# A hybrid decoder layer on one core: splitting 24 of the mixers' weight sets during the first FFN product

## The chip, the core and the metric

The kernel runs on one core of one Trainium2 chip. The metric is the device time of one launch in microseconds (us). A core has five engines with a queue of their own each: TensorE (PE in the profile, its weight loads PEld), VectorE (DVE), ScalarE (ACT), GpSimd (POOL) and SyncE (SP, which here only issues transfers). Each engine works through its own instructions in the order in which they were recorded, and waits where one of them needs something that isn't there yet.

## What is computed

One layer of a decoder trunk on 1024 tokens of width 1024, all in float32:

```python
x = x + 0.5 * swiglu(rms_norm(x, g_ffn1), w1_gate, w1_up, w1_down)      # d_ff 2816
proj = rms_norm(x, g_mix) @ w_in
c_q, k_a, v_a, k_idx, w_idx, q_b, k_b, v_b, gate_a, gate_b = split(proj)
y_a = dsa_attention(...)            # an indexer scores the keys, the best 256 of each row are attended to
y_b = stick_breaking_attention(q_b, k_b, v_b)
merged = sigmoid(gate_a) * (y_a @ w_o_a) + sigmoid(gate_b) * (y_b @ w_o_b)
x = x + merged @ w_out
x = x + 0.5 * swiglu(rms_norm(x, g_ffn2), w2_gate, w2_up, w2_down)
```

Here `w_in` is 1024 x 4104; 512 columns each of it are `q_b`, `k_b` and `v_b`, 1024 each the two gates.

## The kernel before

Products are done in three passes: both factors are split into a high part (rounded to the matmul's format, `fp32r`) and a low part (the rest), and high by high, high by low and low by high are summed in PSUM. So every operand needs a split before its matmul: a rounding copy on ACT and a subtraction on another engine.

**The FFN products** (`ffn_in`, `ffn_out`) use a seven-product scheme of Strassen's kind on 2 x 2 blocks. `ffn_in` goes over 11 pairs of column blocks `p`; from the second pair on each does two calls of `products` (gate and up), each with seven `mul` of 12 matmuls of 128 x 512. For each call SP loads two weight blocks (`a0r`, `a1r`), DVE forms four sums of them (`s1` to `s4`, lines 456 to 459), ACT rounds seven operands (line 377) and POOL subtracts (line 378). Behind the PE, DVE adds the products up in a ring of 12 tiles, `c` (`a0u`, `a0c`, `a1u`, `asg` and so on), and `finish` writes seven of them per pair to DRAM (`staged`, line 591). Here a scheduler orders the instructions.

**The mixers** stand between the two FFNs and are recorded by a planner, `Weave`: each stream of work is a generator that says before a step which engine it wants and what it needs; the planner keeps a time for each engine and each tile from a cost per instruction, takes the step that can start first (ties by rank), and so writes out one fixed order for all engines. It has two stages, `index` and `attend`. Side by side run:

- `indexer` (PE `psdot`, ACT `relu`, DVE `u`): the scores of six row blocks; blocks 0 and 1 need no selection;
- `topk`: the 256th score of each row is searched bit by bit, 31 bits for each of two groups of three blocks, `groups`; a bit is three counting passes on ACT (line 1136, `junka`) and a few small DVE steps. Then per block a mask is made (lines 1181 to 1194: `gt`, `eq`, `cum`) and stored to `bd`;
- `sticks` and `values`: stick-breaking attention (PE `psz`, ACT `left` and `sa`, DVE a scan and a product, PE transposes `pstT`, ACT and DVE `pt`, PE `psy`);
- `logits`, `soft` and `latent_values`: the sparse attention (PE `psL`, DVE `e`, ACT an exponential at line 1757, DVE a division at line 1760, PE transposes `pspT`, then `pso`). The exponential needs another ACT table, which is loaded once, after the last sigmoid of the gates;
- `fillers`, with the lowest rank: the projections of the mixers' other inputs. A weight set is 128 columns of `w_in` for all 1024 rows. There are 8 for `q_b` and `k_b` (`wqk...`) and 16 for the gates (`wg...`), each used by two times 24 matmuls (`psf`); a half of a gate set ends with a sigmoid on ACT (line 1067, `evg`) and a store. Later the output projections `psob` and `psoa` fill in.

Weight sets come through `weights`, at most three at a time: SP loads 512 KB into one of two `raw` tiles (line 971), ACT rounds all of it (line 974), POOL subtracts (line 976) into a ring of four tiles `w`, two for each set.

## Time and profile before

| | us |
|---|---|
| median of 3 runs (2271.07 to 2281.2) | 2272.52 |
| the profiled execution | 2276.41 |
| span of it, first to last instruction | 2274.6 |
| PE busy | 2183.0 (96%) |
| DVE busy | 1576.1 (69%) |
| ACT busy | 1110.5 (49%) |
| POOL busy | 925.9 (41%) |

The profile counts an engine as busy while one of its instructions runs; times in its views are counted from the start of the span. The granted clock is the share of its full speed that the TensorE had. The first FFN product takes the span up to about 440 us, its second half to about 660, the mixers to about 1500, then follow the output projection and the second FFN.

### The profile page before, as it was taken

What the parts mean: (1) busy time and instruction counts of PE and PEld (TensorE: products, weight loads), DVE (VectorE), ACT (ScalarE), POOL (GpSimd) and SP (SyncE); (2) the same over time, 40 slices, a digit from 0 to 9 for tenths busy, and PEclk for the clock granted to TensorE, in tenths of its full rate; (3) what the DMA queues carried; (4) which work ended last, traced back from release to release, by engine and by line L of the source; (5) the groups of instructions that cost most, each with busy time, mean ns of one, the idle gap of its engine ahead of it and who ended that gap; (6) DMA issues with size and microseconds to landing.
All of it is one profiled execution on the core that took longest, in us unless ns stands there. A gap on an engine that the chain in (4) does not pass through costs nothing.

```text
span 2274.6 us, 30225 instructions
## 1 busy us (share of the span) xinstructions
PE 2183.0 (96%) x10460; PEld 1811.1 (80%) x10460; DVE 1576.1 (69%) x2500; ACT 1110.5 (49%) x2145; POOL 925.9 (41%) x722
## 2 busy tenths in 40 slices
PE   7999999999999899899999799999999999999999
PEld 6788888888879788677788578887878888888877
DVE  5765666678863698477788978853477575757775
ACT  4323232334453368899999656633332323233443
POOL 3555555432253444422323132256255555543233
PEclk9999999999999999999999799999999999999999
DMA  5233333587674343655454532467223333358755
GB/s 168 71 116 92 114 95 113 170 293 257 172 204 131 87 130 92 168 126 116 110 135 128 180 109 90 151 203 251 96 67 112 93 113 94 115 172 287 248 160 184
DMA packets 247930, 330.65 MB, mean 145 GB/s; under 512 B 20576, under 2 KB 154352, under 8 KB 247776
## 3 DMA queue, kind: packets, MB, share of 16 engines
q1 hardware_dynamic: 235264, 288.83, 42.3%
q0 software_dynamic: 12512, 39.89, 4.8%
q8 instruction: 82, 1.34, 0.2%
q14 instruction: 72, 0.59, 0.1%
HBM read 234.78 MB, written 93.88 MB: 144 GB/s over the span
## 4 chain that ended last, share of the span: by engine, by line
PE 70%; DVE 10%; DMA 7%; ACT 6%; issue 5%; POOL 2%; SPq 0%; ACTq 0%; DVEq 0%; POOLq 0%
PE p L677 5%; PE p L678 5%; PE p L676 5%; PE pc L467 3%; PE pc L469 3%; PE pc L468 3%; PE pd L469 3%; PE pd L467 3%; PE pd L468 3%; PE pa L469 3%; PE pa L467 3%; PE pa L468 3%; ACT junka L1136 2%; PE pb L467 2%; PE pb L469 2%
## 5 line engine op out<-in xcount | busy, mean ns | idle before, releaser
L1136 ACT ACTIVATE junka<-u,cand,sig 128x768 bf16<-128x768 f32 (+4 forms) x186 | 183.3, 985 | 10.8 <-DVE cand L1133 9.0
L1577 DVE TENSOR_TENSOR_SCAN left<-left 128x640 f32<-128x640 f32 (+3 forms) x64 | 88.1, 1378 | 3.4 <-ACT left L1569 3.3
L1626 DVE TENSOR_TENSOR pt<-pstT,pt 128x512 fp32r<-128x512 f32 (+1 forms) x96 | 51.1, 551 | 24.8 <-ACT pt L1624 24.2
L1580 DVE TENSOR_TENSOR sa<-sa,left 128x639 f32<-128x639 f32 (+3 forms) x64 | 58.6, 918 | 3.7 <-ACT sa L1571 0.4
L1626 DVE TENSOR_TENSOR pt<-pspT,pt 128x512 fp32r<-128x512 f32 x72 | 46.6, 683 | 19.4 <-ACT pt L1624 19.4
L1680 PE MATMUL pstT<-ident,sa 128*128 128x128 f32 x288 | 47.0, 278 | 11.1 <-DVE sa L1580 5.6
L1624 ACT ACTIVATE pt<-pspT 128x512 fp32r<-128x512 f32 x72 | 39.7, 596 | 36.2 <-PE pspT L1836 35.9
L1757 ACT ACTIVATE e<-e,nm 128x256 f32<-128x256 f32 (+7 forms) x64 | 49.4, 774 | 13.0 <-DVE nm L1752 11.3
L677 PE MATMUL p<-bT,bS 128*128 128x512 f32 x132 | 51.9, 393 | 2.7 <-DVE bT L378 2.7
L678 PE MATMUL p<-bT,bS 128*128 128x512 f32 x132 | 51.7, 394 | 1.0 <-POOL bS L378 1.0
L1680 PEld LDWEIGHTS pstT<-ident,sa 128*128 128x128 f32 x288 | 34.7, 141 | 22.4 <-DVE pt L1626 9.0
L677 PE MATMUL p<-aT,aS 128*128 128x512 f32 x132 | 51.6, 391 | 0.8 <-DVE aT L378 0.8
L1745 DVE CUSTOM_DVE_ANT_0 e<-psL,bias 128x512 f32<-128x512 f32 (+3 forms) x96 | 49.7, 550 | 3.8 <-PE psL L1782 3.8
L1836 PE MATMUL pspT<-ident,e 128*128 128x128 f32 x288 | 42.3, 284 | 10.2 <-DVE e L1760 6.1
L1624 ACT ACTIVATE pt<-pstT 128x512 fp32r<-128x512 f32 (+1 forms) x96 | 46.3, 505 | 11.2 <-PE pstT L1680 10.1
L1490 DVE SCALAR_TENSOR_TENSOR u<-relu,WI,u 128x512 f32<-128x512 f32 (+1 forms) x70 | 47.6, 696 | 4.9 <-ACT relu L1483 3.9
L678 PE MATMUL p<-aT,aS 128*128 128x512 f32 x132 | 50.4, 389 | 0.0
L1483 ACT ACTIVATE relu<-psdot 128x512 f32<-128x512 f32 (+1 forms) x80 | 39.9, 520 | 19.0 <-DVE u L1490 10.3
L1836 PEld LDWEIGHTS pspT<-ident,e 128*128 128x128 f32 x288 | 35.2, 145 | 17.5 <-DVE e L1760 8.9
L1569 ACT ACTIVATE left<-psz 128x512 f32<-128x512 f32 (+2 forms) x96 | 45.9, 502 | 5.5 <-PE psz L1604 5.3
L1899 POOL TENSOR_TENSOR o<-o,gate 128x512 f32<-128x512 f32 x16 | 21.8, 1360 | 65.2 <-ACT o L1894 65.2
L1571 ACT ACTIVATE sa<-psz 128x512 f32<-128x512 f32 (+2 forms) x96 | 46.4, 506 | 0.0
(3067 smaller groups left out, 8319.0 us busy)
## 6 DMA issues: line engine op xcount, KB each, us to landing
aw<-in_w_down_dram SPq DMA_DIRECT2D x33, 512.0 KB, 4.7
bw<-in_w_down_dram SPq DMA_DIRECT2D x33, 512.0 KB, 4.7
a0r<-in_w_gate_dram SPq DMA_DIRECT2D x22, 512.0 KB, 4.3
a1r<-in_w_up_dram SPq DMA_DIRECT2D x22, 512.0 KB, 5.0
b0r<-in_w_gate_dram SPq DMA_DIRECT2D x22, 512.0 KB, 4.1
b1r<-in_w_up_dram SPq DMA_DIRECT2D x22, 512.0 KB, 4.9
x<-in_x_dram SPq DMA_DIRECT2D x16, 512.0 KB, 6.4
gd<-evg POOLq DMA_DIRECT2D x32, 256.0 KB, 6.5
```

The costliest lines, as they stand in the source:

```text
L467: nc.tensor.matmul(ps, a[:, c], b[k][:, HI], start=start and k == 0, stop=False, skip_group_check=True)
L468: nc.tensor.matmul(ps, a[:, c], b[k][:, LO], start=False, stop=False, skip_group_check=True)
L469: nc.tensor.matmul(ps, a[:, l], b[k][:, HI], start=False, stop=k == 3, skip_group_check=True)
L676: nc.tensor.matmul(ps[q][m], S[:, h], T[:, HI], start=p == 0, stop=False)
L677: nc.tensor.matmul(ps[q][m], S[:, h], T[:, LO], start=False, stop=False)
L678: nc.tensor.matmul(ps[q][m], S[:, l], T[:, HI], start=False, stop=p == last)
L1136: nc.scalar.activation(junks[1][:, 0:(i + 1) * P], score[i], AF.Sign, scale=sig[:, b:b + 1], bias=cand.bitcast(F32)[:, b:b + 1], accum_out ...
L1577: nc.vector.tensor_tensor_scan(back, back, back, 1.0, op0=ALU.mult, op1=ALU.bypass)
L1624: nc.scalar.activation(pt[:, off:512], tp[:, off:512], AF.Copy)
L1626: nc.vector.tensor_sub(pt[:, 512 + off:1024], tp[:, off:512], f32(pt[:, off:512]))
L1680: nc.tensor.transpose(tp[:, q * P:(q + 1) * P], A[n + q][:, j * P:(j + 1) * P], ident)
L1836: nc.tensor.transpose(tp[:, q * P:(q + 1) * P], E[n + q][:, j * P:(j + 1) * P], ident)
```

## The change

In the first FFN product, `mul` now calls `beside` behind each of the seven products of a call. Over the first 16 of the 20 calls it takes 48 pieces of 128 x 512 (24 sets, two pieces each) in three slots: a piece is loaded behind one product, rounded on ACT and subtracted on DVE behind a later one, and both parts are stored to DRAM behind the next. `behind` makes each of these wait for the given product's last matmul.

The tiles come out of other rings: the ring `c` has 9 tiles instead of 12 in the loop, `s` 5 instead of 7, and six tiles of 128 x 512 carry the three pieces.

In the mixers these 24 sets are no longer rounded and subtracted: `weights` waits for two tiles of the ring `w` and loads both parts, two transfers of 512 KB instead of one. The last set asked for must have taken its tiles first (`before`). The second selection group is (7, 6, 3) instead of (6, 7, 3).

```diff
-    def ffn_in(nm, R, wg, wu, raw, op, sums, ct, bank, staged, rows, first=None):
+    def ffn_in(nm, R, wg, wu, raw, op, sums, ct, bank, staged, rows, first=None, beside=lambda n, ins: None):
...
-                nc.tensor.matmul(ps, a[:, l], b[k][:, HI], start=False, stop=k == 3, skip_group_check=True)
+                ins = nc.tensor.matmul(ps, a[:, l], b[k][:, HI], start=False, stop=k == 3, skip_group_check=True)
+            return ins
...
-            times(O[a], B[b], ps, start)
+            beside("1567243".index(str(n)), times(O[a], B[b], ps, start))
...
-        sums = of(spool, "s", 7, 512)
+        sums, pair = of(spool, "s", 5, 512), of(spool, "pair", 2, 512, F32R)
...
+            c4, c5, c3, c1 = (of(cpool, f"c{n}", n, 512, F32R) for n in (4, 5, 3, 1))
+            ct = fp(in_turn(*[(f, 1) for f in [c4] * 4 + [c5] * 5]))
+            spare = in_turn((c3, 3), (c1, 1), (pair, 2))
...
+            pieces = [(nm, c) for nm in columns for c in range(0, 1024, 512)]
+            held, points = {}, ((0, 1, 3), (2, 3, 5), (4, 5, 0))
...
+            def beside(n, ins):
+
+                for slot, (split_, store, load_) in enumerate(points):
+                    if n == split_ and slot in held:
+                        nm, c, raw, hi = held[slot]
+                        behind(ins, nc.scalar.activation(hi, raw, AF.Copy))
+                        nc.vector.tensor_tensor(raw, raw, f32(hi), op=ALU.subtract)
+                    if n == store and slot in held:
+                        nm, c, raw, hi = held.pop(slot)
+                        behind(ins, *(nc.sync.dma_start(d[:, c:c + 512], part)
+                                      for d, part in zip(split_of[nm], (f32(hi), raw))))
+                    if n == load_ and pieces:
+                        nm, c = pieces.pop(0)
+                        raw, hi = f32(spare(f"swr{slot}")), spare(f"swh{slot}")
+                        held[slot] = nm, c, raw, hi
+                        behind(ins, nc.sync.dma_start(raw.rearrange("p (k f) -> p k f", f=P),
+                                                      rows_of[:, c // P:(c + 512) // P, columns[nm]:columns[nm] + P]))
...
-    groups = ((5, 4, 2), (6, 7, 3))
+    groups = ((5, 4, 2), (7, 6, 3))
...
+                if nm in split_of:
+                    yield SP, (ws, 2), before
+                    W.parts = ws(nm + "h"), ws(nm + "l")
+                    mark("got" + nm)
+                    for wp, part in zip(W.parts, split_of[nm]):
+                        nc.sync.dma_start(f32(wp), part)
+                    return
```

The planner writes another order for all engines. Three places of it follow. Line numbers in the changed kernel are higher by 1 in `finish`, and by 46 or 47 in the mixers.

ACT, at the end of the search. `junka` is a counting pass of the search, `evg` the sigmoid of a half gate set, `pt` with `pstT` belongs to the sticks, `e` is the exponential. Before:

```order
L1136 ACTIVATE junka,cnt_6038<-u_7809,cand_6043,sig_6039 128x512
L1624 ACTIVATE pt<-pstT 128x384
L974 ACTIVATE ob2h<-ob2r 128x1024
L1624 ACTIVATE pt<-pstT 128x256
L1067 ACTIVATE evg<-psf 128x512
L1624 ACTIVATE pt<-pstT 128x128
L1624 ACTIVATE pt<-pstT 128x512
L1633 ACTIVATE yl<-psy 64x512
L1624 ACTIVATE pt<-pstT 128x384
L1624 ACTIVATE pt<-pstT 128x256
L1639 ACTIVATE yh<-yl 64x512
L1624 ACTIVATE pt<-pstT 128x128
```

After, the last pass stands behind all work of the sticks:

```order
L1183 ACTIVATE junka,cnt_6422<-u_8161,cand_6427,sig_6423 128x512
L1686 ACTIVATE yh<-yl 64x512
L1114 ACTIVATE evg<-psf 128x512
L1228 ACTIVATE gt,cnt_6422<-u_7571,fix_11970 128x1024
L1114 ACTIVATE evg<-psf 128x512
L1020 ACTIVATE ob0h<-ob0r 128x1024
L1114 ACTIVATE evg<-psf 128x512 x2
L1228 ACTIVATE gt,cnt_6422<-u_7882,fix_11970 128x896
L1020 ACTIVATE ob2h<-ob2r 128x1024
L1114 ACTIVATE evg<-psf 128x512
L1802 ACT_TABLE_LOAD
L1804 ACTIVATE e,ssum<-e,nm 128x256 x6
```

In the first list the table load comes next. Before, one sigmoid of a gate stood behind the last search pass, now there are five, and two of the three masks of the second group (`gt` of 1024 and of 896 columns) stand ahead of the first exponential.

PE, between the second and the third group of the sparse attention's transposes. Before, the rows from the products `pso` on:

```order
L1816 MATMUL pso<-pt,kkh 128x512
L1817 MATMUL pso<-pt,kkl 128x512
L1818 MATMUL pso<-pt,kkh 128x512
L1781 MATMUL psL<-kkh,qs 128x256
L1782 MATMUL psL<-kkl,qs 128x256
L1836 MATMUL pspT<-ident,e 128x128 x4
```

After, the first twelve of the rows from the same products on:

```order
L1863 MATMUL pso<-pt,kkh 128x512
L1864 MATMUL pso<-pt,kkl 128x512
L1865 MATMUL pso<-pt,kkh 128x512
L1828 MATMUL psL<-kkh,qs 128x256
L1829 MATMUL psL<-kkl,qs 128x256
L308 MATMUL psob<-ybh_12174,ob0h 128x512
L309 MATMUL psob<-ybl_12178,ob0h 128x512
L310 MATMUL psob<-ybh_12174,ob0l 128x512
L308 MATMUL psob<-ybh_12175,ob0h 128x512
L309 MATMUL psob<-ybl_12179,ob0h 128x512
L310 MATMUL psob<-ybh_12175,ob0l 128x512
L308 MATMUL psob<-ybh_12176,ob0h 128x512
```

Among the first 24 transposes of the sparse attention there are now 33 matmuls of the output projection `psob`, where there were none.

SP in the first FFN product: loads of the weights (`a1r`, `a0r`) and stores of the products. Before, for one pair:

```order
L440 DMA a1r_1461<-in_w_up_dram 128x8x128
L440 DMA a1r_1463<-in_w_up_dram 128x8x128
L440 DMA a0r_1606<-in_w_gate_dram 128x8x128
L440 DMA a0r_1608<-in_w_gate_dram 128x8x128
L591 DMA staged_82<-a0u_1134 128x512
L591 DMA staged_82<-asg 128x512
L591 DMA staged_82<-a0c_1161 128x512
```

After, a stretch of the same pair; `swr` is a piece of a mixers' set, `wg12hd` and `wg12ld` are its two parts in DRAM:

```order
L790 DMA wg11ld<-swr_1225 128x512
L440 DMA a0r_1772<-in_w_gate_dram 128x8x128
L796 DMA swr_1381<-in_w_in_dram 128x4x128
L790 DMA wg12hd<-swh_1260 128x512
L790 DMA wg12ld<-swr_1259 128x512
L440 DMA a0r_1774<-in_w_gate_dram 128x8x128
L592 DMA staged_82<-a0u_1230 128x512
L592 DMA staged_82<-asg 128x512
L796 DMA swr_1415<-in_w_in_dram 128x4x128
L790 DMA wg12hd<-swh_1333 128x512
L790 DMA wg12ld<-swr_1332 128x512
L592 DMA staged_82<-a0c_1264 128x512
```

Loads and stores of the pieces now stand between the loads of the FFN's own weights and between the stores of its products: 18 more transfers for each pair, where there were 11.

## Rows read from the trace of the kernel before

**Rows 1.** The page, part 1: busy us (share of the span) and instructions of each engine.

```profile
PE 2183.0 (96%) x10460; PEld 1811.1 (80%) x10460; DVE 1576.1 (69%) x2500; ACT 1110.5 (49%) x2145; POOL 925.9 (41%) x722
```

**Rows 2.** Windows: length, busy PE, PEld, DVE, ACT, POOL; granted clock, DMA share, GB/s.

```profile
100.00:440.00 340.00, 340.00 (x1501) 281.51 (x1501) 218.13 (x235) 104.44 (x181) 183.93 (x127) 1.00 0.35 111
...
400.00:500.00 100.00, 99.65 (x440) 82.21 (x439) 68.72 (x89) 32.12 (x56) 37.57 (x23) 1.00 0.66 221
...
842.00:1264.00 422.00, 398.77 (x2033) 322.80 (x2033) 319.42 (x584) 384.76 (x816) 134.74 (x140) 0.98 0.50 131
1264.00:1280.00 16.00, 7.42 (x37) 5.87 (x36) 15.45 (x58) 9.00 (x22) 3.98 (x5) 0.79 0.56 200
...
1279.00:1313.00 34.00, 25.03 (x82) 17.91 (x82) 30.60 (x111) 16.75 (x46) 2.17 (x4) 0.65 0.32 95
```

**Rows 3.** Windows of lines 974 (ACT) and 976 (POOL) alone: busy, count.

```profile
842.00:1264.00 422.00, 24.45 (x23) 0.98 0.50 131
...
842.00:1264.00 422.00, 60.78 (x23) 0.98 0.50 131
```

**Rows 4.** Groups of ACT by line, 842 to 1264 us: busy, mean ns, idle before.

```profile
L1136 ACT ACTIVATE junka<-u,cand,sig 128x768 bf16<-128x768 f32 (+4 forms) x186 | 183.3, 985 | 10.8 <-DVE cand L1133 9.0
...
L1624 ACT ACTIVATE pt<-pstT 128x512 fp32r<-128x512 f32 (+1 forms) x91 | 44.2, 509 | 4.8 <-PE pstT L1680 3.8 <-DVE pt L1626 0.8
...
L1067 ACT ACTIVATE evg<-psf 128x512 f32<-128x512 f32 x31 | 18.6, 599 | 0.1
```

**Rows 5.** Timeline of PE: start, duration, instruction [idle before, releaser].

```profile
1250.16 0.39 PE L308 MATMUL psf<-mhi,wg7h 128*128 128x512 f32 x1
...
1250.84 0.39 PE L308 MATMUL psf<-mhi,wg7h 128*128 128x512 f32 x1
...
1268.93 0.66 PE L1680 MATMUL pstT<-ident,sa 128*128 128x128 f32 x4 [3.89 <-DVE pt L1626]
...
1279.59 0.96 PE L1836 MATMUL pspT<-ident,e 128*128 128x128 f32 x2 [4.05 <-DVE nm L1752]
```

**Rows 6.** Timeline of ACT: the last search pass and the table load.

```profile
1261.86 0.89 ACT L1136 ACTIVATE junka<-u,cand,sig 128x512 bf16<-128x512 f32 x1
...
1274.39 1.28 ACT L1755 ACT_TABLE_LOAD   x1
```

**Rows 7.** Groups of DVE and PE by line, 1280 to 1320 us.

```profile
L1187 DVE TENSOR_TENSOR_SCAN cum<-eq 128x896 f16<-128x896 f16 (+2 forms) x3 | 5.5, 1838 | 0.0
...
L1190 DVE TENSOR_TENSOR eq<-cum,gt 128x896 f16<-128x896 f16 (+2 forms) x3 | 1.7, 576 | 0.0
...
L1836 PE MATMUL pspT<-ident,e 128*128 128x128 f32 x24 | 7.6, 417 | 10.2 <-DVE e L1760 6.1 <-DVE nm L1752 4.0
```

**Rows 8.** Timeline of PE, where the fillers' first rounded set comes in.

```profile
764.71 0.80 PE L310 MATMUL psf<-mhi,wqk5200l 128*128 128x512 f32 x1 [3.00 <-POOL wqk5200l L976]
...
769.36 0.60 PE L1400 MATMUL pskt<-ident,kdup 128*128 128x128 f32 x4
...
786.83 0.79 PE L1513 MATMUL psdot<-kih,qsi 128*128 128x512 f32 x1 [6.45 <-ACT relu L1483]
```

**Rows 9.** Timeline of DVE and of the SP queue in the first FFN product.

```profile
193.83 0.69 DVE L458 TENSOR_TENSOR a05s<-a0r,a0r 128x512 f32<-128x512 f32 x1
...
201.35 1.77 DVE L459 TENSOR_TENSOR a05s<-a0r,a05s 128x512 f32<-128x512 f32 x1
...
214.28 0.68 DVE L493 TENSOR_TENSOR a0c<-a0u,pc 128x512 f32<-128x512 f32 x1
...
205.45 0.32 SPq L591 DMA_DIRECT2D staged<-a0u  x1
```

**Rows 10.** DMA issues: line, engine, count, KB each, median us from issue to landing.

```profile
staged<-a0u SPq DMA_DIRECT2D x20, 256.0 KB, 4.0
...
qs<-qad SPq DMA_DIRECT2D x8, 512.0 KB, 4.6
...
wg9r<-in_w_in_dram SPq DMA_DIRECT2D x1, 512.0 KB, 16.8
```

More of the change, by code (lines that the diff above doesn't have):

```diff
@@ L722, in trunk @@
     bd = dram.tile([P, 4224], BF16, name="bd")
+    columns = {f"wg{g}": C_GA + g * P for g in (*range(ND, 2 * ND), *range(ND))}
+    columns.update((f"wqk{base}{pr}", base + pr * P) for pr in range(4) for base in (C_QB, C_KB))
+    split_of = {nm: [dram.tile([P, 1024], F32, name=f"{nm}{part}d") for part in "hl"] for nm in columns}
+    rows_of = w_in[0].rearrange("(k p) f -> p k f", p=P)
     put_high, put_low = nc.scalar.dma_start, nc.gpsimd.dma_start
@@ L785, in trunk @@
             R.second = lambda: R.place(xs[4:8], 1, sums)
-            ffn_in("a", R, w1_gate, w1_up, raw, op, sums, ct, bank, staged[0], range(4), first)
+            ffn_in("a", R, w1_gate, w1_up, raw, op, sums, ct, bank, staged[0], range(4), first, beside)
+            assert not held and not pieces
         hpool.append(tc.tile_pool(name="hpool", bufs=1, side="right"))
@@ L873, in trunk @@
         aux = of(pool, "u", 8, 512)
+        sums = in_turn((sums, 5), (lambda name: f32(pair(name)), 2))
         ffn_out("a", xs, w1_down, raw, op, sums, aux, bank, staged[0], after)
@@ L971, in stream @@
                 nc.sync.dma_start(rv, w[0, k0 * P:(k0 + k) * P, c0:c0 + n].rearrange("(k p) f -> p k f", p=P))
-                yield ACT, raw, (ws, 2)
+                yield ACT, raw, (ws, 2), before
                 wh, wl = ws(nm + "h"), ws(nm + "l")
+                mark("got" + nm)
                 nc.scalar.activation(wh[:, 0:m], raw[:, 0:m], AF.Copy)
@@ L987, in __init__ @@
             def __init__(self, *of):
-                self.todo, self.coming = list(of), []
+                self.todo, self.coming, self.last = list(of), [], None
             def __call__(self):
                 while self.todo and len(self.coming) < 3:
-                    self.coming.append(weights(*self.todo.pop(0)))
+                    last, self.last = self.last, "got" + self.todo[0][-1]
+                    self.coming.append(weights(*self.todo.pop(0), before=last))
                 return self.coming.pop(0)
```

11 lines of the change are left out of this document (7 added, 4 removed).

## The prediction

> **What bounds the kernel now.** I read the page's first part, then windows by stage, then groups and timelines in the stages that the change touches. The PE is busy 96% of the span [rows 1], so a change that leaves its work alone can only win the time in which PE waits or runs at the lower clock. The windows [rows 2] say where that is. In the first FFN product there is none: from 100 to 440 us PE is busy 340.00 of 340 us at full clock, beside DVE 218, ACT 104 and POOL 184. In the mixers there is some. From 842 us (the first counting pass) to 1264 (behind the last) PE is busy 398.8 of 422 us; ACT, with 384.8 us or 91%, is nearly as full, and the search alone takes 183.3 us of it [rows 4]. Behind the last search pass comes a hole: PE is busy 7.4 of 16 us from 1264 to 1280, and from 1279 to 1313 it runs 25.0 of 34 us at a granted clock of 0.65, so that much of that time was at 1.2 GHz instead of 2.4. The reader is to see two things there. The sticks have run out just as the search ends, so PE waits for single results (3.89 us for a `pt`, 4.05 us for the first exponentials [rows 5]). And in the small blocks that follow, PE waits 10.2 us for DVE [rows 7], which is busy 30.6 of 34 us, among other things with the masks of the second group.
>
> **What the change removes.** From 842 to 1264 us ACT rounds 23 sets in 24.45 us, 1.06 us each, and POOL subtracts 23 in 60.78 us, 2.64 us each [rows 3]. Twenty of the 23 are of the 24 sets; the others belong to `wvb` and `ob`. So 20 x 1.06 = 21 us leave ACT in the stretch in which it is 91% full. The other four sets lie before 842 us and count in the second term below.
>
> **First term, the FFN product: 0.** Added are 48 copies on ACT (0.6 us each by the `evg` of [rows 4], an operation of the same 128 x 512, so 29 us), 48 subtractions on DVE, and 144 transfers with 37.7 MB. The work that hides them is PE's: it has no gap in 340 us. Sixteen calls of 19 us (half of the pair's 38) are 305 us, in which DVE has 64% = 196 us of its own work. A subtraction of two SBUF tiles of this size takes 0.69 us, or 1.77 us when POOL works beside it [rows 9]; so the addition is 33 to 85 us, and DVE comes to 75% to 92%. ACT comes to 40%. The traffic rises from 111 GB/s by 124 to about 235; the second half of the FFN moves 221 GB/s with PE at 99.65% [rows 2]. The Trainium skill (SBUF — State Buffer, Who interferes with whom) speaks against the change here: a two-input DVE operation and a POOL operation take the shared ports in turn, each for its whole length. The trace agrees as far as it goes (0.69 against 1.77 us); by that rule alone all 48 would cost the upper price, DVE would stand at 92%, and the term would still be 0. If the cover is gone, each microsecond that a pair's work comes late costs 10 us, once for each of the ten pairs; that is a rival below.
>
> **Second term, the fillers' first set: +3 us.** Now the first `psf` waits 3.00 us for POOL's subtraction [rows 8]. In the changed kernel the set's tiles are free only when the last products with `wvb` have read them, at about 760 us, and then two transfers of 512 KB must land. The nearest row is 4.6 us for 512 KB [rows 10], so PE waits until some 765 to 767 us, and six fillers and six `psq` that stood ahead of the transposes `pskt` now stand behind them, which wait for a DVE result until 769.36 us anyway. Twelve matmuls at 0.227 us are 2.7 us moved behind. Below it is bounded by 0, if the later wait of 6.45 us at 780 us, behind a store, swallows it; above by 6.
>
> **Third term, from the first search pass to the first exponential: -6 us.** ACT's work to the last search pass changes by -21 us, by 7 more `pt` that now stand ahead of it (+3.6 us at 0.51), by 4 sigmoids fewer (-2.4 us at 0.60), and by three copies of the sticks' outputs more (+1.8, priced alike): 384.8 falls to about 367 us. At the same 91% that is 402 us instead of 422, so the last pass, now at 1261.9 us [rows 6], ends about 20 us earlier, near 1244. But behind it stand five half gates instead of one. A half is 24 matmuls 0.227 us apart ((1250.84 - 1250.16) / 3 [rows 5]), 5.4 us; with part of one done, 4.5 x 5.4 = 24.3 us. Then come the table load and the way from it to the first transposes, 1279.59 - 1274.39 = 5.2 us [rows 5, 6]. 1244 + 24.3 + 5.2 = 1273.5, against 1279.6: -6 us. The PE's own work allows it: 406 us busy from 842 to 1280, and one half set of `q_b` or `k_b` more (+5.4), make 1254 without any wait, so the lower bound of the term is -21 us (5 us of waits left). The upper bound is +14: if the search does not end earlier, 1264 + 24.3 + 5.2 = 1293.5.
>
> **Fourth term, the small blocks: -14 us.** From 1279 to 1313 us PE does 82 matmuls in 34 us. Busy 25.0 us at clock 0.65 is worth 16 us at full clock (estimate: product of the two), so 18 us are lost. In the new order 33 matmuls of `psob` stand among the same transposes, 33 x 0.227 = 7.5 us, so PE has 23.5 us to do. DVE had 30.6 us there; two of the second group's three masks are now made ahead of it, under the gates' matmuls, which takes off two thirds of 5.5 + 1.7 us [rows 7], 5 us. DVE then needs about 25.5 us, and I take 27 for the stretch: 3.5 us lost instead of 18, -14.5. Bounds: -18 if nothing is lost, -5 if DVE still sets the pace of the first transposes and PE falls back to the lower clock.
>
> **Sum.** 0 + 3 - 6 - 14 = -17 us on the profiled execution's 2276.4, so 2259.4. That execution lies 3.9 us above the median of the runs shown, 2272.5; on the median the forecast is 2255.5. What lies behind 1313 us keeps its order of transposes and fillers and its work, and I leave it at 0, as the swap of blocks 6 and 7, which keeps each pass and mask.
>
> **Rivals.** *The search keeps its time* (no change). The bits form a chain, pass, compare, next bit, and if that chain and not ACT's load sets the end, the third term is +14: 3 + 14 - 14 = +3, 2275. For it: the passes are spread over the whole stretch. Against: they wait for DVE only 9.0 us in all [rows 4], and ACT is 91% busy. Chance 0.15.
>
> *The sets come late* (a smaller gain). They are now asked for only when the set before last has been used, and with more bytes in flight; one of the old loads took 16.8 us [rows 10]. A set lasts PE 10.9 us in the dense run at the end of the gates. With 17 us per set the last two there would each stall PE 6 us: -17 + 12 = -5, 2267. Against: 4.6 us for the like [rows 10]. Chance 0.08.
>
> *PE becomes the limit* (a larger gain). If ACT was not the only brake and DVE, freed of 20 POOL subtractions of 2.64 us beside it, delivers sooner, the third term goes to -19, the fourth to -17, the second to 0: -36, 2236. The same page of the Trainium skill says so: POOL's hold of the ports falls away. For it: the same kind of operation took 1.77 us instead of 0.69 [rows 9]. Against: DVE is only 76% busy in the stretch. Chance 0.14.
>
> *The FFN product stalls* (slower). The ring `c` has 9 tiles, so the third tile that a pair takes is the one that the pair before gives back with its last store. Now that store is issued at 205.45 us, lands 4.0 us later, and its tile would be wanted at 214.28 [rows 9, 10]: 4.8 us to spare. In the new order two loads and four stores of pieces stand between a pair's stores on SP ahead of it, each with a wait, and SP holds all behind a waiting one. If it lands 4.8 + 4 us later, DVE stands 4 us in each of ten pairs, and with DVE the evacuation of PSUM: +40 - 17 = +23, 2295. It decides from 2.8 us per pair on (28 us, which leaves +11). The Trainium skill (DMA: Bandwidth & Descriptors, Anatomy of one DMA) has the same mechanism: a wait is spent on the issuing sequencer before dispatch. For it also: SP's order shows it. Against: the waits are for products that end at about the times at which SP stood idle there, and the sums of pair 5's weights are formed at 193.83 us, 20 us before the gate product of pair 4 is added up at 214.28 [rows 9]. Chance 0.09.
>
> **How the numbers follow.** The forecast has 0.54; its own range is 2247 to 2264, from the second and fourth terms' bounds and half of the third's. About 0.5% (11 us) is what a measurement of this kernel can tell from no change, so faster means below 2261. Of the forecast 0.46 lies there and 0.08 within the bound; with the larger gain faster has 0.60, with the search and the late sets no change has 0.31, slower 0.09. For 8 in 10 the range takes in the larger gain but for its tail and the search rival: 2237 to 2277.
>
> **What would show it.** The 100 to 440 us window with PE still 100% and DVE above 75%; no rounding of `wqk` and `wg` sets; the last search pass 15 to 25 us earlier than 1262; a dense run of gate matmuls behind it; the first `pspT` a few microseconds earlier; the 34 us of small blocks down to about 27, at a clock above 0.65. Wrong it would be if PE shows gaps in the FFN product, if the last pass stays near 1262, or if PE waits for the sets' transfers.

## The result, and the profile of the changed kernel

The changed kernel takes 2260.69 us (median of 5 runs, 2258.06 to 2263.85) against 2272.52 before: the medians are 11.8 us (0.52%) apart, and the ratio taken over all runs is 0.9938, 95% interval 0.9916 to 0.9961. The forecast was 2255.5 with 2247 to 2264 as its own range. The total came out near it by luck: the first term was 33 us too low, the second and third together 29 us too high.

The profiled execution spans 2262.1 us (2263.85 with what lies around it), before 2274.6. The page of the changed kernel begins as [rows 1] did:

```profile
PE 2172.7 (96%) x10460; PEld 1804.9 (80%) x10460; DVE 1581.0 (70%) x2548; ACT 1110.2 (49%) x2169; POOL 865.4 (38%) x698
```

DVE has its 48 subtractions more, and ACT and POOL have lost the 24 roundings and subtractions of whole sets (ACT has 48 smaller ones instead). The totals of PE, DVE and ACT hardly move; where the time lies has moved. Windows of the changed kernel, columns as in [rows 2]:

```profile
100.00:440.00 340.00, 316.01 (x1353) 256.47 (x1352) 228.04 (x256) 117.86 (x211) 167.06 (x114) 0.98 0.70 205
...
863.00:1251.00 388.00, 377.72 (x1989) 310.82 (x1988) 302.78 (x617) 365.33 (x799) 81.12 (x120) 0.99 0.54 163
...
1280.00:1314.00 34.00, 29.94 (x158) 25.08 (x158) 29.41 (x116) 21.37 (x55) 12.59 (x13) 0.95 0.60 196
```

The first line is the surprise. PE, busy 340.00 of 340 us before [rows 2], now stands for 24 of the same 340 us, while none of its engines is full (DVE 67%, ACT 35%, POOL 49%, transfers 70%). The second line is the search: the window is 388 us long where it was 422, with PE at 97% and ACT at 94%. The last line is the small blocks: at a clock of 0.95 instead of 0.65, PE does 158 matmuls in the time of 82.

To put a number on each stage, four events are read in each kernel: the last sum of the FFN product that takes in `pb` (`a1u<-a1u,pb`), the first and last counting pass of the search (`junka`), and the first transposed exponentials (`pspT`). For the first of them the view by tile gives, before the change and after it (count, shortest, median and longest duration in ns, first and last start):

```profile
L484 DVE TENSOR_TENSOR a1u<-a1u,pb x10: 686/687/689, 107.1 to 449.8; 128x512 f32<-128x512 f32 x10
```

```profile
L485 DVE TENSOR_TENSOR a1u<-a1u,pb x10: 672/674/686, 112.8 to 483.2; 128x512 f32<-128x512 f32 x10
```

The last of the ten moved from 449.8 to 483.2: the FFN product ends 33.4 us late. The other events of the changed kernel, from the timelines of ACT and of PE:

```profile
1248.77 0.80 ACT L1183 ACTIVATE junka<-u,cand,sig 128x512 bf16<-128x512 f32 x1
```

```profile
1280.61 1.94 PE L1883 MATMUL pspT<-ident,e 128*128 128x128 f32 x8 [5.50 <-DVE ri L1806]
```

With 842.0 and 863.0 us for the first pass (before, after) the spans split as follows; the differences add up to the difference of the spans, -12.5 us.

| stretch, us | before | after | difference | forecast |
|---|---|---|---|---|
| start to last `a1u` sum of the FFN product | 449.8 | 483.2 | +33.4 | 0 |
| from there to the first search pass | 392.2 | 379.8 | -12.4 | +3 |
| first search pass to first `pspT` | 437.6 | 417.6 | -20.0 | -6 |
| first `pspT` to the end | 995.0 | 981.5 | -13.5 | -14 |

What PE waits for between 80 and 490 us (engine, tile, line, then who ended the wait: us in total, times, longest):

```profile
PE pc L467 <- DVE a0u L489: 16.4, 8, 4.8
PE pc L467 <- DVE a1u L489: 7.4, 5, 3.8
```

PE wants to put its sixth product into the bank `pc`, and DVE (line 489) hasn't yet added up what lies there. DVE in turn waits, in the same stretch, at line 456, where the next gate and up weights (`a0r`, `a1r`) are first used; the view of that line says how long its engine stood before it:

```profile
  DMA a1r<-in_w_up_dram: 46.9, 8
  DMA a0r<-in_w_gate_dram: 35.8, 7
```

DVE had such waits before the change too, with PE standing 2.9 us in the same stretch, so by themselves they cost it little:

```profile
  DMA a1r<-in_w_up_dram: 41.6, 9
  DMA a0r<-in_w_gate_dram: 25.4, 8
```

PE loses more than the waits. All of them from 80 us on come to 26.3 us, 23.4 more than before; the rest of the 33.4 us is PE at work: about as many matmuls up to the last `a1u` sum (1617 each) keep it busy for 376.9 us instead of 366.9, at a mean granted clock of 0.98 instead of 1.00. Behind the 4.82 us wait below its matmuls start 0.43 us apart instead of 0.227, the lower of its two clock levels (1.2 instead of 2.4 GHz), and the granted clock of 266 to 274 us is 0.57:

```profile
267.94 0.80 PE L467 MATMUL pc<-aT,a05A 128*128 128x512 f32 x1 [4.82 <-DVE a0u L489]
...
268.96 0.63 PE L469 MATMUL pc<-aT,a05A 128*128 128x512 f32 x1
269.39 0.63 PE L467 MATMUL pc<-aT,a05A 128*128 128x512 f32 x1
```

Now a place in the fourth pair, SP's queue first, then DVE, then PE (start, duration, instruction, [idle before it and who ended it]). Before the change, the second half of the same load and DVE's first sum with it:

```profile
149.96 0.37 SPq L440 DMA_DIRECT2D a0r<-in_w_gate_dram  x1
```

```profile
154.49 0.69 DVE L456 TENSOR_TENSOR a04s<-a0r 128x512 f32<-128x512 f32 x1 [3.20 <-DMA a0r<-in_w_gate_dram]
```

After it:

```profile
158.62 0.38 SPq L440 DMA_DIRECT2D a0r<-in_w_gate_dram  x1
159.12 0.52 SPq L796 DMA_DIRECT2D swr<-in_w_in_dram  x1
159.68 0.50 SPq L790 DMA_DIRECT2D wg12hd<-swh  x1
160.88 0.34 SPq L790 DMA_DIRECT2D wg12ld<-swr  x1
161.32 0.42 SPq L440 DMA_DIRECT2D a0r<-in_w_gate_dram  x1
```

```profile
168.63 1.25 DVE L456 TENSOR_TENSOR a04s<-a0r 128x512 f32<-128x512 f32 x1 [4.54 <-DMA a0r<-in_w_gate_dram]
...
173.21 0.68 DVE L787 TENSOR_TENSOR swr<-swr,swh 128x512 f32<-128x512 f32 x1
...
180.81 0.68 DVE L787 TENSOR_TENSOR swr<-swr,swh 128x512 f32<-128x512 f32 x1
181.42 0.67 DVE L489 TENSOR_TENSOR a0u<-a0u,pc 128x512 f32<-128x512 f32 x1
```

```profile
182.15 0.50 PE L467 MATMUL pc<-aT,a03A 128*128 128x512 f32 x1 [1.31 <-DVE a0u L489]
```

Three transfers of pieces stand in SP's order between the two halves of one weight load. They don't part the halves here: 2.7 us lie between them, as before the change (147.25 and 149.96 us). But the second half has landed only at 168.6, 7.3 us behind its issue, where it took 4.5; DVE starts its sums of weights the later, has two subtractions of pieces in the run that follows (1.2 us together, the second directly ahead of the sum that PE needs), and PE stands 1.31 us. So two things take part here, the bytes of the pieces and the subtractions on DVE. DVE also stands for the pieces themselves: before a subtraction it waits for ACT's rounding, and ACT for its product or for the piece:

```profile
DVE swr L787 <- ACT swh L786: 20.4, 14, 6.2
```

The third is the pieces' place in SP's order. SP itself waits for them: a load of a piece (line 796) waits until the slot's earlier piece has been stored. The two longest of sixteen such rows, which come to 62.6 us:

```profile
SPq L796 <- DMA wg0ld<-swr: 9.8, 2, 8.0
...
SPq L796 <- DMA wg6ld<-swr: 6.2, 1, 6.2
```

### The profile page after: what moved, and what is told of

It reads as the page before. It is cut to its first block, busy times and chain, and to the rows that moved or that the text cites. A ratio compares the mean times of both kernels' runs of the same rounds, so it can differ in the third digit from the quotient of the medians.

```text
span 2262.1 us, 30632 instructions
## 1 busy us (share of the span) xinstructions
PE 2172.7 (96%) x10460; PEld 1804.9 (80%) x10460; DVE 1581.0 (70%) x2548; ACT 1110.2 (49%) x2169; POOL 865.4 (38%) x698
## 4 chain that ended last, share of the span: by engine, by line
PE 61%; DVE 8%; ACT 7%; issue 4%; DMA 3%; POOL 1%; SPq 0%; ACTq 0%; DVEq 0%; POOLq 0%
PE p L678 5%; PE p L679 5%; PE p L677 5%; ACT junka L1183 4%; PE pc L467 2%; PE pc L468 2%; PE pc L469 2%; PE pd L469 2%; PE pd L467 2%; PE pd L468 2%; PE pa L469 2%; PE pa L467 2%; PE pa L468 2%; PE psf L308 2%; PE psf L310 2%
## 5 line engine op out<-in xcount | busy, mean ns | idle before, releaser
L1117 POOL DMA_DIRECT2D gd<-evg x32 | 17.9, 558 | 152.5 <-ACT evg L1114 112.6
L787 DVE TENSOR_TENSOR swr<-swr,swh 128x512 f32<-128x512 f32 x48 | 47.2, 984 | 25.4 <-ACT swh L786 20.4
L786 ACT ACTIVATE swh<-swr 128x512 fp32r<-128x512 f32 x48 | 29.9, 624 | 62.9 <-PE pa L469 14.3
L1627 DVE TENSOR_TENSOR sa<-sa,left 128x639 f32<-128x639 f32 (+3 forms) x64 | 48.1, 752 | 3.7 <-ACT sa L1618 0.2
L1530 ACT ACTIVATE relu<-psdot 128x512 f32<-128x512 f32 (+1 forms) x80 | 40.1, 520 | 17.7 <-DVE u L1537 8.7
L1618 ACT ACTIVATE sa<-psz 128x512 f32<-128x512 f32 (+2 forms) x96 | 46.9, 510 | 0.1
```

## The experiments

Twelve kernels were run. Lateness is that of the last `a1u` sum against 449.8 us; times with an interval are medians of several runs on a chip on which the kernel before also ran (its medians there are 2272.5 to 2274.5), the others single runs.

| kernel | time, us | ratio to before | lateness | last `a1u` sum to first pass | search | search to `pspT` | `pspT` to end |
|---|---|---|---|---|---|---|---|
| before | 2272.5 | 1 | 0 | 392.2 | 419.9 | 17.7 | 995.0 |
| changed | 2260.7 | 0.9938 (0.9916 to 0.9961) | 33.4 | 379.8 | 385.8 | 31.8 | 981.5 |
| spread points | 2247.4 | 0.9879 (0.9856 to 0.9902) | 16.5 | 380.1 | 386.3 | 31.9 | 983.9 |
| transfers only | 2249.2 | | 16.9 | 378.3 | 386.2 | 31.8 | 984.1 |
| splitting only | 2235.9 | | 2.1 | 380.4 | 386.0 | 31.8 | 984.0 |
| no pieces | 2230.0 | 0.9809 (0.9792 to 0.9827) | 0.2 | 376.1 | 386.1 | 31.7 | 984.3 |
| spread, no pace | 2301.4 | | 68.8 | 378.4 | 385.9 | 31.9 | 984.8 |
| spread, ACT and GpSimd issue | 2271.7 | 0.999 (0.9979 to 1.0001) | 43.2 | 378.1 | 386.0 | 31.8 | 980.4 |
| spread, ACT issues | 2269.7 | 0.9984 (0.9969 to 0.9999) | 39.4 | 378.9 | 386.0 | 31.8 | 983.8 |
| spread, small transfers | 2231.6 | | 1.3 | 376.1 | 386.4 | 31.8 | 984.4 |
| quiet points | 2249.6 | 0.9888 (0.9872 to 0.9905) | 21.4 | 376.1 | 386.1 | 31.8 | 983.0 |
| spread, ACT's roundings back | 2266.0 | | 17.7 | 380.6 | 407.9 | 16.0 | 992.3 |
| spread, GpSimd's subtractions back | 2262.8 | | 16.8 | 385.9 | 390.6 | 37.8 | 980.1 |
| two slots, 20 sets | 2253.8 | 0.9918 (0.99 to 0.9935) | 15.9 | 383.1 | 389.1 | 31.1 | 978.7 |

**Four kernels on the FFN product.** The first moves the points:

```diff
-            held, points = {}, ((0, 1, 3), (2, 3, 5), (4, 5, 0))
+            held, points = {}, ((0, 1, 4), (2, 3, 6), (4, 5, 1))
```

> Same transfers, same work; only the points move, so that a piece's load stands four or three products (8 to 11 us) behind the stores that free its tiles instead of two (5.4 us). Reading of the changed kernel: the last FFN sum of the first product (a1u<-a1u,pb) ends its series at 483.2 us instead of 449.8, 33.4 us late, and SP's loads of pieces wait some 60 us in all for a store of the slot's earlier piece to land. Theory A (the queue: a load that waits for its slot's store holds SP, and the next pair's gate and up weights come late behind it): SP's waits on stores all but vanish, the lateness falls to under 12 us, the time to about 2238 us. Theory B (traffic: the bytes make every transfer land later, whatever stands in what order): no change, 483 and 2261. Theory C (the 48 subtractions on DVE stand ahead of the sums that PE waits for): no change, 483 and 2261.

The lateness fell to 16.5 us and the time to 2247.4: between what theory A (waits on SP) and what B (bytes) and C (subtractions on DVE) said. SP's waits of a piece's load for a store fell from 62.6 us to 5.7, in six rows of which this is the longest; what is left of the pieces' waits on SP is mostly for the products at which they are paced (44 us in all) and for their own splitting.

```profile
SPq L796 <- DMA wg6ld<-swr: 1.5, 1, 1.5
```

The second leaves out the splitting, the third the transfers, the fourth both:

```diff
-                        behind(ins, nc.scalar.activation(hi, raw, AF.Copy))
-                        nc.vector.tensor_tensor(raw, raw, f32(hi), op=ALU.subtract)
+                        pass
...
-                                      for d, part in zip(split_of[nm], (f32(hi), raw))))
+                                      for d, part in zip(split_of[nm], (raw, raw))))
```

> Leaves out the rounding and the subtraction of the pieces; the unsplit piece is stored twice, so the transfers and their points stay. Theory A: most of the 33.4 us stays, 470 to 483 for the last a1u sum, 2248 to 2261 us; A's waits on stores remain. Theory B: the same. Theory C: the lateness goes, 450 to 455, about 2230 us.

```diff
-    split_of = {nm: [dram.tile([P, 1024], F32, name=f"{nm}{part}d") for part in "hl"] for nm in columns}
+    one = [dram.tile([P, 1024], F32, name=f"one{part}d") for part in "hl"]
+    split_of = {nm: one for nm in columns}
...
+                        if nm == "wg8":
+                            behind(ins, *(nc.sync.dma_start(d[:, c:c + 512], part)
+                                          for d, part in zip(split_of[nm], (f32(hi), raw))))
...
+                        if slot not in kept:
...
+                            nc.sync.dma_start(raw.rearrange("p (k f) -> p k f", f=P), rows_of[:, 0:4, columns[nm]:columns[nm] + P])
+                        held[slot] = (nm, c, *kept[slot])
```

> Leaves out the transfers of all pieces but the first set's stores and one load per slot; 48 roundings and 48 subtractions stay at their points, on three resident pieces, and every set of the mixers is read from the one stored set (the same bytes in the mixers). Theory A and theory B: the lateness goes, 450 to 456, about 2230 us. Theory C: it stays, 475 to 483, about 2255 us.

```diff
-    split_of = {nm: [dram.tile([P, 1024], F32, name=f"{nm}{part}d") for part in "hl"] for nm in columns}
+    one = [dram.tile([P, 1024], F32, name=f"one{part}d") for part in "hl"]
+    split_of = {nm: one for nm in columns}
...
-            pieces = [(nm, c) for nm in columns for c in range(0, 1024, 512)]
+            pieces = [(nm, c) for nm in ["wg8"] for c in range(0, 1024, 512)]
```

> Leaves out all pieces but the two of the first set; every set of the mixers is read from that one stored set, so the mixers do the same work and move the same bytes. It prices the mixers' side alone. All theories: PE full from 100 to 440 us, the last a1u sum at about 450. If the gain of the mixers (12 us before the search, 20 in it, 14 in the small blocks, read from the two traces) stands on its own, the time is about 2272.5 - 46 = 2227 us. If part of it is only waits of the FFN product made up later (work that was late anyway finds the search emptier), the gain is smaller: at 30 us, 2243.

Splitting without the transfers is nearly free: 2.1 us late. Its window has DVE at 80% and PE full:

```profile
100.00:440.00 340.00, 339.81 (x1490) 278.70 (x1490) 270.78 (x283) 125.94 (x223) 186.92 (x126) 1.00 0.36 111
```

Theory C by itself falls. But the transfers without the splitting cost 16.9 us, not 33.4 (less than A and B said), although SP's waits of loads for stores are all there (76.0 us) and DVE stands longer for the weights: 71.4 and 52.3 us at line 456 (46.9 and 35.8 in the changed kernel).

```profile
  DMA a1r<-in_w_up_dram: 71.4, 9
  DMA a0r<-in_w_gate_dram: 52.3, 8
```

So a late weight load costs PE more when DVE has the subtractions to do as well. Whether that is the subtractions' own time or their waits for late pieces isn't separated: with resident pieces the longest such wait is 1.2 us, in the changed kernel 6.2. The costs don't add: transfers 16.9, splitting 2.1, both 33.4. Without either, the kernel takes 2230.0 us, where the kernel before took 2273.5 on the same chip: this is the mixers' gain by itself, 43.5 us against the 17 that were forecast, and it stands on its own. This kernel has the changed kernel's smaller rings too, so 9 tiles in `c` and 5 in `s` cost nothing without the pieces.

**Bytes or order.** Four more kernels start from the spread points.

```diff
-                        behind(ins, *(nc.sync.dma_start(d[:, c:c + 512], part)
-                                      for d, part in zip(split_of[nm], (f32(hi), raw))))
+                        for d, part in zip(split_of[nm], (f32(hi), raw)):
+                            nc.sync.dma_start(d[:, c:c + 512], part)
...
-                        behind(ins, nc.sync.dma_start(raw.rearrange("p (k f) -> p k f", f=P),
-                                                      rows_of[:, c // P:(c + 512) // P, columns[nm]:columns[nm] + P]))
+                        nc.sync.dma_start(raw.rearrange("p (k f) -> p k f", f=P),
+                                          rows_of[:, c // P:(c + 512) // P, columns[nm]:columns[nm] + P])
```

> The spread points, with the order of SP unchanged, but loads and stores of pieces no longer wait for a product (only the rounding does); they wait for their data alone. The spread points alone left the last a1u sum at 466.3 us, 16.5 late, with 57 us of SP's waits on products. Theory A (SP held by waits, now by the pace): a good part goes, 455 to 460, about 2240 us. Theory B (the bytes make the transfers land late): 466 or a little more, 2247 us.

This went against both, 68.8 us late, and its premise was wrong: without the pace the scheduler puts the pieces' transfers earlier in SP's order, so the order did change. (SP's waits on products in the spread kernel, too, are 44 us by the view and not 57.) What it shows is theory A in a strong dose. On SP's timeline the second half of a weight load leaves 7.8 us behind the first, because the piece's load between them waits 6.8 us for a store:

```profile
229.46 0.42 SPq L440 DMA_DIRECT2D a1r<-in_w_up_dram  x1
236.73 0.38 SPq L796 DMA_DIRECT2D swr<-in_w_in_dram  x1
237.21 0.45 SPq L440 DMA_DIRECT2D a1r<-in_w_up_dram  x1
```

```profile
SPq L796 <- DMA wg0ld<-swr: 6.8, 1, 6.8
```

Next, the issue was taken off SP (`put_high` is ACT's `dma_start`, `put_low` GpSimd's):

```diff
-                        behind(ins, *(nc.sync.dma_start(d[:, c:c + 512], part)
-                                      for d, part in zip(split_of[nm], (f32(hi), raw))))
+                        behind(ins, *(put(d[:, c:c + 512], part) for put, d, part in
+                                      zip((put_high, put_low), split_of[nm], (f32(hi), raw))))
...
-                        behind(ins, nc.sync.dma_start(raw.rearrange("p (k f) -> p k f", f=P),
+                        behind(ins, put_high(raw.rearrange("p (k f) -> p k f", f=P),
```

> The spread points, but the pieces' loads and high stores are issued by ACT and the low stores by GpSimd, so that SP carries only the FFN's own transfers; bytes, work and points unchanged. Theory A: SP is free, the last a1u sum comes at 450 to 455, about 2233 us. Theory B: no gain, about 466, 2247 us. A rival to both: ACT's and GpSimd's own waits for products and stores now hold the halves of the operands, then the lateness is moved to the operand tiles and the time is 2245 or more.

The other has `nc.scalar.dma_start` for all three transfers.

> As the run before, with all three transfers of a piece issued by ACT. ACT then also waits for DVE's subtraction before each low store. Theory A: 450 to 458, 2233 to 2240 us. Theory B: 466, 2247 us. If ACT's waits count: over 466.

Both are later than with SP as the issuer, by 27 and 23 us (43.2 and 39.4 against 16.5), so A alone is out, and the outcome is the third reading's. Where ACT issues everything, the trace shows it: a low store waits for DVE's subtraction, and the rounding of an operand that stands behind the store on ACT (line 377) waits with it. There are sixteen such waits, 64.0 us in all, and none in the spread kernel; one of them:

```profile
156.62 0.63 ACT L377 ACTIVATE a03A<-a0r 128x512 fp32r<-128x512 f32 x1 [4.19 <-DVE swr L787]
```

For the kernel in which GpSimd has a share the place of the loss wasn't traced. In the kernel in which ACT issues everything, SP isn't free either: its weight loads waited 40.2 us for pieces' loads.

```profile
SPq L440 <- DMA swr<-in_w_in_dram: 40.2, 7, 8.8
```

The Trainium skill (DMA: Bandwidth & Descriptors, Rules for kernel authors) says that spreading transfers over the issuing engines brings no bandwidth, since all run on the same 16 engines, and saves issue time only. These two runs agree as far as no bandwidth was gained (198 and 200 GB/s from 100 to 440 us, 208 in the spread kernel), and add that the waits that come with a transfer move with its issue.

The last of the four keeps SP's order and its waits for products and takes away the bytes; every set of the mixers is read from the one that is stored whole:

```diff
...
+                        w = 512 if nm == "wg8" else 32
-                        behind(ins, *(nc.sync.dma_start(d[:, c:c + 512], part)
+                        behind(ins, *(nc.sync.dma_start(d[:, c:c + w], part[:, 0:w])
...
+                        raw, hi = kept[slot]
+                        held[slot] = nm, c, raw, hi
+                        behind(ins, nc.sync.dma_start(raw[:, 0:32], rows_of[:, c // P, columns[nm]:columns[nm] + 32]))
```

> The spread points with every transfer of a piece on SP at its place and with its waits, but 32 columns wide instead of 512 (a sixteenth of the bytes; each slot's first load and the first set's stores are whole, and every set of the mixers is read from that set); rounding and subtraction whole. Theory A: SP is held as before, 460 to 466 for the last a1u sum, about 2245 us. Theory B: the lateness goes, 450 to 454, about 2232 us.

1.3 us late, PE full, with as many transfers on SP as in the spread kernel. Theory B holds for what the spread points left over: it needs the bytes. With them go late weights and late pieces alike, so this run doesn't tell which of the two makes DVE late. The view of the DMA issues from 80 to 440 us (KB each, median us to landing), first of the changed kernel, then of this one; before the change the weights landed in 4.2 and 4.9 us:

```profile
swr<-in_w_in_dram SPq DMA_DIRECT2D x48, 256.0 KB, 5.8
a0r<-in_w_gate_dram SPq DMA_DIRECT2D x18, 512.0 KB, 4.9
a1r<-in_w_up_dram SPq DMA_DIRECT2D x18, 512.0 KB, 6.4
```

```profile
a1r<-in_w_up_dram SPq DMA_DIRECT2D x18, 512.0 KB, 4.6
a0r<-in_w_gate_dram SPq DMA_DIRECT2D x17, 512.0 KB, 3.9
```

**Keeping the bytes away from the weights.** One line again:

```diff
-            held, points = {}, ((0, 1, 4), (2, 3, 6), (4, 5, 1))
+            held, points = {}, ((3, 5, 1), (4, 5, 1), (5, 6, 2))
```

> All 24 sets on SP as in the spread kernel; the points now leave free the stretch of a call in which the next gate or up weights are asked for and land (from the end of its fourth product to the end of its sixth): loads behind the second and third product, stores behind the sixth and seventh, so the two weight loads stand side by side in SP's order with no transfer of a piece between them. Bytes, rounding and subtraction unchanged. If the loss of the spread kernel (last a1u sum at 466.3, 16.5 us late) is the sharing of the transfer engines just while the weights land: 450 to 457, about 2235 us. If it is the mean traffic, wherever it stands: 462 to 470, 2245 to 2250 us. A rival: the six transfers and two splittings that now come in clusters hold SP or DVE longer at one place; then over 470.

21.4 us late: the weight loads now stand side by side in SP's order, and it doesn't help. The same view gives 5.4 us for `a0r`, but 8.3 for `a1r` and 7.6 for the pieces' loads, which now come in a cluster just ahead of `a1r`. The sum at 471.2 us lies just above the 470 of the rival with the clusters, the time within that of the mean traffic; the two aren't told apart.

The last run took a third of the bytes out of each call:

```diff
-    columns = {f"wg{g}": C_GA + g * P for g in (*range(ND, 2 * ND), *range(ND))}
+    columns = {f"wg{g}": C_GA + g * P for g in (*range(ND, 2 * ND), *range(ND - 4))}
...
-            held, points = {}, ((0, 1, 4), (2, 3, 6), (4, 5, 1))
+            held, points = {}, ((3, 5, 1), (5, 6, 1))
```

> Two pieces per call instead of three, over all 20 calls: 40 pieces, so 20 of the 24 sets are split in the FFN product (120 transfers of 256 KB over twenty calls instead of 144 over sixteen: a third fewer in each), and the last four gates' sets (wg4 to wg7) go the old way in the mixers; stores behind the sixth and seventh product, loads behind the second, away from the weights' loads. If the remaining 16 to 21 us of the spread and the quiet kernel are the bytes per call, the last a1u sum comes at 451 to 458 (1 to 8 us late), and with some 4 us for the four sets' work in the mixers the time is 2236 to 2242 us, the fastest of all correct ones. If the subtractions' place on DVE makes it, a third less of them: 461 to 464, about 2245 us.

15.9 us late, where at most 8 were expected if the bytes per call were all. But here the sum is a poor yardstick: from 80 us to it PE did 1647 matmuls, 30 more than before the change (about 6.8 us), so at equal work it was 9 us late, near what was expected, and stood 5.2 us more in the last pair, where pieces still come. A place in the second pair shows one kind of wait that is left: a piece's load leaves at 129.58 us, ACT, which has the rounding next in its order, stands 12.5 us for it, DVE stands 5.4 us for ACT with the subtraction, and the sum behind it (line 490) lets PE stand 3.7 us.

```profile
129.58 0.39 SPq L796 DMA_DIRECT2D swr<-in_w_in_dram  x1
```

```profile
138.91 0.63 ACT L786 ACTIVATE swh<-swr 128x512 fp32r<-128x512 f32 x1 [12.52 <-DMA swr<-in_w_in_dram]
```

```profile
139.57 0.69 DVE L787 TENSOR_TENSOR swr<-swr,swh 128x512 f32<-128x512 f32 x1 [5.44 <-ACT swh L786]
140.18 0.68 DVE L490 TENSOR_TENSOR a0u<-a0u,pd 128x512 f32<-128x512 f32 x1
```

```profile
140.92 0.50 PE L467 MATMUL pd<-aB,a02S 128*128 128x512 f32 x1 [3.72 <-DVE a0u L490]
```

No arrangement tried brings the sum in under 15.9 us late with the transfers whole; whether one exists stays open. The spread points give the fastest complete kernel of this study, 2247.4 us, which its interval doesn't set apart from the quiet points.

**Two kernels on the mixers.** Each puts one part of the removed work back behind the sets' loads.

```diff
                     for wp, part in zip(W.parts, split_of[nm]):
                         nc.sync.dma_start(f32(wp), part)
+                    yield ACT, *W.parts
+                    nc.scalar.activation(W.parts[0], f32(W.parts[0]), AF.Copy)
```

> The spread kernel, with each of the 24 sets rounded once more by ACT behind its load in the mixers (values unchanged), so ACT's old work there comes back and GpSimd's does not. The planner then orders the mixers anew. In the spread kernel the search takes 386.3 us from its first pass to its last (419.9 before the change). If the removed ACT work made the gain: 404 to 412, and 2255 to 2268 us. If the removed GpSimd subtractions made it: 386 to 392, about 2248 us.

```diff
                     for wp, part in zip(W.parts, split_of[nm]):
                         nc.sync.dma_start(f32(wp), part)
+                    yield POOL, *W.parts
+                    nc.gpsimd.tensor_tensor(W.parts[1], f32(W.parts[1]), f32(W.parts[0]), op=ALU.subtract)
```

> The spread kernel, with GpSimd subtracting the high from the low part of each of the 24 sets once more behind its load in the mixers (this changes the low parts), so GpSimd's old work and the wait for it come back and ACT's does not. The planner then orders the mixers anew. If the removed ACT work made the gain of the search: 386 to 390 us from its first pass to its last, about 2248 us. If the removed GpSimd work made 14 us of it (the rival of a larger gain): about 400 us and 2258 to 2262 us.

The length of the search is ACT's: with the roundings back it takes 407.9 us instead of 386.3, as expected; with GpSimd's subtractions back 390.6, just above the 386 to 390 expected if ACT made the gain. But the whole span grew by 12.5 us with GpSimd's work too (by 15.8 with ACT's), 5.8 us of it ahead of the search and 5.9 behind it. The planner's new order hides where PE lost the time. Windows of the search in the spread kernel and with GpSimd's work, columns as in [rows 2]:

```profile
846.40:1232.70 386.30, 375.66 (x1979) 308.87 (x1978) 301.57 (x608) 364.37 (x796) 80.27 (x118) 0.99 0.54 163
```

```profile
852.50:1243.10 390.60, 368.39 (x1915) 303.17 (x1914) 326.70 (x576) 360.76 (x783) 123.28 (x133) 0.98 0.50 155
```

PE stands 22.2 us in the search instead of 10.6 and does 64 matmuls fewer in it; they now stand ahead of the search (1973 instead of 1945, with PE standing 10.4 instead of 10.1 us there) and behind it, where seven `pt` of the sticks stand beside the five half gates. So 4.3 us is what GpSimd's work adds to the length of the search, and 11.6 what it adds to PE's waits there. What that work does to DVE is to be seen in the groups of DVE during the search, of the kernel before, of the changed kernel and of the one with GpSimd's work: the widest subtraction `sa` took 2195 ns on average before, 1223 in the changed kernel and 1769 with the work back; all eight widths together (63 or 64 operations) took 58.1, 48.1 and 57.9 us.

```profile
L1580 DVE TENSOR_TENSOR sa<-sa,left 128x1023 f32<-128x1023 f32 x8 | 17.6, 2195 | 0.7
```

```profile
L1627 DVE TENSOR_TENSOR sa<-sa,left 128x1023 f32<-128x1023 f32 x8 | 9.8, 1223 | 0.6
```

```profile
L1629 DVE TENSOR_TENSOR sa<-sa,left 128x1023 f32<-128x1023 f32 x8 | 14.2, 1769 | 0.6
```

## Why the prediction was right in sum, and where it was not

**The range.** The bounds that it names add up to 2241 to 2278, not to 2247 to 2264; the measured 2260.7 lies in both.

**First term (0; measured +33.4): this step failed.** "The work that hides them is PE's" took the engines' shares for the measure: DVE below 92%, ACT at 40%, traffic at a rate that another stage bears. The shares stayed below the forecast (DVE 67%, 205 GB/s), and PE stood all the same: the gaps in the FFN product that the prediction named as its own sign of being wrong. The row that was not read is DVE's wait for the weights: 67 us in this stretch before the change, 3 to 5 for each load, so its loads had no slack. Now they land later (4.9 and 6.4 us behind their issue instead of 4.2 and 4.9), and on an engine that works in order that moves every later operation of the pair. About 10 of the 33.4 us are not waits but PE busy for longer, in good part at the lower clock behind its waits; the prediction had no term for that. The rival *the FFN product stalls* had the outcome and a price of the right size (+40), with 0.09; its mechanism was right only in part. SP does hold the next transfers behind a waiting one, and the spread points, which remove those waits, gave 16.9 us back. The ring `c`, on which the rival rested, doesn't show: no wait of ACT or DVE in these pairs is ended by a pair's stores, and with the same rings but without the pieces the product is 0.2 us late. The other half needs the pieces' bytes (the small transfers removed it). The splitting is needed for the whole loss too, since without it, at the changed kernel's points, 16.9 us are left.

**Second term (+3; measured -12.4): wrong sign.** The forecast moved twelve matmuls behind a late set and put the later wait of 6.45 us [rows 8] down as something that could at most swallow the 3. In the changed kernel that wait is gone. Windows of the stretch, before and after:

```profile
449.80:842.00 392.20, 374.32 (x1970) 320.42 (x1969) 280.21 (x438) 171.13 (x329) 151.54 (x133) 0.99 0.60 184
```

```profile
483.20:863.00 379.80, 368.80 (x1944) 315.83 (x1943) 276.20 (x440) 166.65 (x325) 141.63 (x127) 0.99 0.61 192
```

PE stands 11.0 us instead of 17.9. The other 5.5 us are no gain in themselves: 26 matmuls fewer, mostly of the fillers, stand ahead of the first pass, and come behind it.

**Third term (-6; measured -20.0): right mechanism, wrong size.** The last pass was to come 20 us earlier and the way behind it to grow by 14. The way grew by 14.1 (17.7 to 31.8 us). The search shrank by 34.1. The step at fault is "at the same 91%": ACT's work fell as forecast (365.3 us in the window, 367 forecast), but its share rose to 94%. Of the search's length the roundings put back account for 21.6 us, the subtractions for 4.3; the remaining 8 are not separated from the planner's new order.

**Fourth term (-14; measured -13.5): right.** The clock rows bear it out: 0.95 instead of 0.65 for PE in the 34 us behind the first `pspT`, with `psob` matmuls among the transposes. The same 4472 matmuls from there to the end keep PE busy for 959.8 us instead of 970.5, so 10.7 of the 13.5 us are matmuls done in less time. Part of it hangs on ACT's roundings: with them back, this stretch is 8.4 us longer, and only two half gates instead of five stand behind the last pass (16.0 us from it to `pspT`), so the third and fourth terms hang together through the planner's order.

**The rivals.** *PE becomes the limit* had -19, -17 and 0 for terms three, four and two; measured -20.0, -13.5 and -12.4. It was the better forecast of the mixers, at 0.14. That GpSimd's hold on DVE's operations falls away is true by the rows of `sa`, and the Trainium skill's rule on the shared ports (SBUF — State Buffer, Who interferes with whom) agrees with them; put back, GpSimd's subtractions cost 12.5 us of the whole span (their hold on DVE and the waits for them together), against 15.8 for ACT's roundings, so neither is the whole. *The search keeps its time* and *the sets come late* didn't happen: in the search PE's longest wait for a set's transfer was 0.6 us, and ahead of it the first set cost 2.7. The swap of blocks 6 and 7 was not tried alone.

So 33.4 us lost where nothing was to be lost, and 45.9 won where 17 were forecast, gave a sum 4.5 us from the one forecast (-12.5 against -17): luck, as two errors of some 30 us nearly cancelled. Of the 45.9 us, PE's waits make 25.7 and the same 8510 matmuls done in less time 20.2.

## What to carry to other kernels

A stage with PE at 100% can still be one late transfer away from standing: look at what the engines that feed it wait for, and not only at how full they are. Work put into such a stage behind fixed points brings its own waits into in-order queues, and these hold the stage's own transfers and sums; give each piece's load, split and store more time than a loaded transfer takes, which here was one line and 13 us. And when a sum of terms comes out right, check the terms: without the stage by stage comparison this change would have been filed as a forecast that held.

## What the runs showed that was not expected

Cost was far from additive: 16.9 us for the transfers alone, 2.1 for the splitting alone, 33.4 for both. Moving the issue of 144 transfers from SP to ACT cost 23 us. When PE began to stand in the FFN product, it also lost clock: its waits grew by 23.4 us, and the other 10 of the 33.4 are matmuls that took longer. And the DVE subtractions `sa` took 58.1, 57.9 and 48.1 us in all, in the order of how long GpSimd was busy in the search: 135 of 422 us before the change [rows 2], 123 of 391 with its subtractions put back, 81 of 388 in the changed kernel. The widths didn't gain alike: of the 895 columns one took 1329, 1080 and 1086 ns.
